# A two-layer decoder trunk on one core: where the softmax probabilities are transposed

## The chip, the cores and the metric

One core of one Trainium2 chip. The metric is device microseconds of one execution; the kernel before takes 770.55 us (median of 3 runs, 770.55 to 770.92).

## The reference

Two decoder layers over 528 tokens (16 meta tokens ahead of 512) of width 1024. Each layer normalises, makes one wide projection, and runs two token mixers side by side: a causal pooling and a latent attention with 8 heads. What this case turns on is the attention:

```
s = einsum('bqhd,bkhd->bhqk', q, k) * scale          # head width 96
s = where(causal, s, -1e30)
p = softmax(s, axis=-1)
o = einsum('bhqk,bkhd->bqhd', p, v)                  # value width 64
y_mla = (o * silu(z_mla)) @ w_mla_up
x = x + (sigmoid(g_pool) * y_pool + sigmoid(g_mla) * y_mla) @ w_out
```

Everything is float32.

## The kernel before, in words

**Products in three passes.** A float32 operand is split into a high part that TensorE takes in one pass (`fp32r`) and a low part, the rest. `split` (L274) does it: ScalarE copies the high part (L275), VectorE subtracts (L276). `mm3` (L180) then multiplies high by high, high by low and low by high (L181 to L183). Weights come in chunks of 128x512: `wload` (L170) fetches a chunk by SyncE's DMA queue (SP, L114) into one of three `raw` tiles and splits it (L176 ScalarE, L177 VectorE) into one of three pairs `whi`, `wlo`.

**Two streams of work.** All projections of both layers are listed in `register`, in order, and `stream` (L190) is a generator that emits them piece by piece. Each piece reports planned nanoseconds. Activations lie with the feature on the partitions and the 528 tokens along a row, in two segments of 264 (layer 0) or one of 512 (layer 1, which drops the meta tokens). `go` (L1073) walks through a layer's special parts and between them draws from the stream: `gap` (L1070) draws `FILL` planned ns (2950 in layer 0, 2850 in layer 1), but stops at the projection `RESERVE` (`gm5`); `fill_now` draws a given amount. During the heads the stream holds the tiles of z_mla (4), g_pool (8) and g_mla (8), each of two chunks, each evacuated by VectorE and ScalarE (L549 to L552, L617 to L619, L971 and L972). The framework's scheduler then orders the instructions of each engine, so neighbours in the code may be shifted against each other; on each engine the order is fixed when the kernel is built.

**A head.** `prep` (L735) makes keys and queries of a head (VectorE L742 and L753, GpSimd L743, ScalarE L749, two DMAs L756, one broadcast load L733). `head` (L759) computes the scores of four blocks of 128 queries, with the queries on the partitions. `top` (L774) is a VectorE instruction that adds the mask, scales and finds each row's extreme; `expo` (L781) is ScalarE's exponential, which also sums the row. VectorE adds and inverts the sums (L826, L827). GpSimd multiplies the probabilities by the inverse: the 16 columns of the meta keys into `pm` (L832), the rest in place (L834).

The value product needs the keys on the partitions. `pv` (L837) has TensorE transpose ten 128x128 blocks a head against an identity (L859), three to seven into one PSUM tile; `split` takes them out of PSUM as `th` and `tl`. Four key blocks follow, each a product with both parts of the values (`both`, L872) and one with the low part of the probabilities (`low`, L876), 512, 384, 256 and 128 columns long. `hosts` slips the last scores of the next head between these products in layer 0. The meta columns of two heads are turned by four small VectorE transposes (L848) and split into the three 32-row bands of `racc` (L903 to L905). After an odd head, `part2` adds the product with the meta values (L922), multiplies by the gate `zms` (L926) and splits the result for the up projection.

`pv(prev)` of one head runs in three parts inside the next head's turn: the loop in `go` is `head(h)`, gap, `prep(h+1)`, rest of `pv(h-1)`, gap, with two more gaps inside `head`.

**Tiles.** Probabilities lie in `pa` (two buffers) and in `cq8` to `cq11` by odd and even head; squares for the norms in 16 tiles `sq`; PSUM has four `mm` tiles, three `S` tiles and one `o` tile.

Of the kernel before, what the change touches and what calls it, by code (L numbers as in the profile page):

```python
# [52 lines left out]
FILL = (2950.0, 2850.0)  # L53
RESERVE = ("gm5", "gm5")
# [3 lines left out]
WARM = 8  # L58

# [12 lines left out]
def trunk(ctx, tc, xT, xrow, mrow, pos, win, wkr, wqb, wkb, wvb, wgr, wpu, wmu, wout, gains, const, yT):  # L72
# [23 lines left out]
    def sqt():  # L96
        return tp.tile([P, HALF], F32, tag="sq", name=nm("sq"), bufs=16)
# [72 lines left out]
    def wload(src, n, spare):  # L170
        raw = early.pop(0) if early else fetch(src, n, rawt(), sp)
        loads[0] += 1
        pool, th, tl, nb = (tp, "th", "tl", 2) if loads[0] <= 2 or spare else (wp, "whi", "wlo", 3)
        hi = pool.tile([P, W if pool is tp else 512], F32R, tag=th, name=nm("whi"), bufs=nb)
        lo = pool.tile([P, W if pool is tp else 512], F32R, tag=tl, name=nm("wlo"), bufs=nb)
        act.activation(hi[:, :n], raw[:, :n], AF.Copy)  # L176
        dve.tensor_sub(lo[:, :n], raw[:, :n], hi[:, :n].bitcast(F32))  # L177
        return hi, lo
# [134 lines left out]
    kdr = [dp.tile([H, T], F32, name=f"kdr{l}") for l in range(DEPTH)]  # L313

    hbuf = [(slot(f"hh{k}", F32R), slot(f"hl{k}", F32R)) for k in range(8)]

    class Layer:
        def __init__(self, l):
# [11 lines left out]
            self.sq = []  # L330
# [147 lines left out]
        def kr_rest(self, a, b):  # L478
# [5 lines left out]
            q = sqt()  # L484
# [82 lines left out]
        def mix(self, m, s):  # L567
# [7 lines left out]
            t = "tl" if m % 2 else "th"  # L575
            self.ys[m] = (slot(f"u{m}", F32R), tp.tile([P, W], F32R, tag=t, name=nm(t), bufs=2))
# [46 lines left out]
        def ev_k(self, p):  # L623
            def ev(ps, a, b):
# [6 lines left out]
                q = self.ksq[:, a:b] if p < 3 else sqt()[:, :b - a]  # L631
# [5 lines left out]
        def v_body(self, k, w):  # L637
# [17 lines left out]
            ps = mmt()  # L655
            for k in range(2):
                r = slot("pa", F32R, bufs=2, w=416)[:, 0:4 * NM].rearrange("p (a b) -> p a b", a=4)
# [18 lines left out]
        def q_stat(self, ps, a, b, c):  # L676
            for a0, b0 in FULL:
                a0, b0 = max(a, a0), min(b, b0)
                if a0 < b0:
                    q = sqt()  # L680
# [78 lines left out]
        def head(self, h, kq, prev):  # L759
# [7 lines left out]
            rs = sm.tile([P, 5], F32, tag="rs", name=nm("rs"), bufs=2)  # L767

# [17 lines left out]
            first = scores(1, s1, 0, 272)  # L786
            if self.hosted is not None:
                follow(first, self.hosted)
            scores(3, s3, 0, SPL)
            tops = [top(1, 1, s1, causal(272)), top(3, 4, s3, maskw[:, 0:SPL])]  # L790
# [3 lines left out]
            self.tops = tops + [top(2, 2, s2, causal(400))]  # L794
# [9 lines left out]
            scores(3, s4, SPL, T)  # L804
            def passes(out, q0, n):
# [3 lines left out]
            if self.last:  # L809
                scores(0, s0, 0, 144)  # L810
            else:
                sm_ = sc[0:NM, 432:432 + NM]
                todo = passes(s0, slice(NM, NM + P), 144) + passes(sm_, slice(0, NM), NM)
                if prev is None:
                    for fn in todo:
                        fn()
                else:
                    self.pv(prev, 1, todo)
# [6 lines left out]
            expo(0, 0, s0, pt[0])  # L825
            dve.tensor_add(rs[:, 3:4], rs[:, 3:4], rs[:, 4:5])  # L826
            dve.reciprocal(rs[:, 0:4], rs[:, 0:4])  # L827
            if odd == 0:
                self.pm = sm.tile([P, 4, 32], F32, tag="pm", name=nm("pm"), bufs=2)
# [7 lines left out]
        def pv(self, prev, part, hosts=()):  # L837
# [41 lines left out]
            def chain(*fns):  # L879
                last = None  # L880
                for fn in fns:
                    ins = fn()
                    if last is not None:
                        follow(ins, last)
# [332 lines left out]
```

## Time and profile before

| | |
|---|---|
| median of 3 runs | 770.55 us |
| span of the profiled execution | 768.5 us (its own time is not listed) |
| TensorE busy | 763.8 us |
| VectorE busy | 544.1 us |
| ScalarE busy | 408.9 us |
| GpSimd busy | 201.6 us |
| data moved by DMA | 84.05 MB, 109 GB/s |
| granted TensorE clock | 9 tenths or more of full speed in all 40 slices |

Times are microseconds of one profiled execution unless marked ns. PE is TensorE's matmuls, PEld its weight loads, DVE VectorE, ACT ScalarE, POOL GpSimd, SP or SPq SyncE with its DMA queue. L859 is line 859 of the kernel. A group is all instructions of one line, engine and shape: how many, their summed busy time, the mean of one in ns, then the idle time of the engine just before them and what ended it. A matmul's record runs from its start to its modelled end, and matmuls overlap: the price of one is the distance of starts. The chain that ended last is followed back from the last instruction, at each step to what released it.

### The profile page before, as it was taken

The numbers are of one execution on the slowest core, as the hardware profiler recorded it, in microseconds if no ns is written. First come the engines' busy times: TensorE is split into PE (matmuls) and PEld (weight loads), VectorE is DVE, ScalarE is ACT, GpSimd is POOL, SyncE is SP. The second block draws the span as 40 slices with busy tenths as digits, with TensorE's granted clock in tenths as the row PEclk, the third lists the DMA queues.
The fourth block names the chain that finished last, engine by engine and source line by source line (L and its number), as shares of the span: only waits on it lengthen the run. The fifth ranks groups of instructions, "written<-read, shape, count | busy, mean of one in ns | idle before, by whom it ended". The sixth has DMA issues, their size and how long they took to land.

```text
span 768.5 us, 14355 instructions
## 1 busy us (share of the span) xinstructions
PE 763.8 (99%) x5195; PEld 697.9 (91%) x5195; DVE 544.1 (71%) x1179; ACT 408.9 (53%) x892; POOL 201.6 (26%) x251
## 2 busy tenths in 40 slices
PE   9999999999999999999999999999999999999998
PEld 9999999999999999999997898887888888888887
DVE  5588687357899977785376486773677989775842
ACT  6755656545556665634264355454446666664320
POOL 2026204012242233052220262040132434420500
PEclk9999999999999999999999999999999999999999
DMA  8533233343223222325642333334433332222372
GB/s 293 160 113 98 75 97 98 104 141 105 89 79 91 84 71 70 107 71 169 178 133 97 110 86 89 96 87 127 125 119 90 94 93 77 82 69 70 119 222 98
DMA packets 54931, 84.05 MB, mean 109 GB/s; under 512 B 10006, under 2 KB 18582, under 8 KB 54860
## 3 DMA queue, kind: packets, MB, share of 16 engines
q1 hardware_dynamic: 54716, 82.87, 35.6%
q8 instruction: 41, 0.67, 0.4%
q14 instruction: 30, 0.25, 0.1%
q10 hardware_dynamic: 144, 0.26, 0.1%
HBM read 76.69 MB, written 4.29 MB: 105 GB/s over the span
## 4 chain that ended last, share of the span: by engine, by line
PE 99%; DMA 0%; ACT 0%; DVE 0%; SPq 0%; issue 0%; ACTq 0%
PE mm L181 29%; PE mm L183 29%; PE mm L182 29%; PE mm L859 2%; PE S L181 2%; PE S L182 2%; PE S L183 2%; PE o L876 1%; PE o L872 1%; PE S L503 1%; PE S L470 0%; DMA xb<-xT 0%; PE S L806 0%; PE mm L922 0%; PE mm L395 0%; PE S L872 0%
## 5 line engine op out<-in xcount | busy, mean ns | idle before, releaser
L181 PE MATMUL mm<-hh,whi 128*128 128x264 f32 (+2 forms) x1080 | 339.9, 317 | 0.0
L182 PE MATMUL mm<-hl,whi 128*128 128x264 f32 (+2 forms) x1080 | 338.2, 314 | 0.0
L183 PE MATMUL mm<-hh,wlo 128*128 128x264 f32 (+2 forms) x1080 | 337.1, 315 | 0.0
L177 DVE TENSOR_TENSOR wlo<-raw,whi 128x512 fp32r<-128x512 f32 (+2 forms) x251 | 186.7, 748 | 98.6 <-ACT whi L176 94.6
L176 ACT ACTIVATE whi<-raw 128x512 fp32r<-128x512 f32 (+2 forms) x251 | 150.2, 602 | 181.3 <-PE mm L182 135.3
L181 PEld LDWEIGHTS mm<-hh,whi 128*128 128x128 f32 x1080 | 202.5, 188 | 12.9 <-ACT kp L474 0.4
L182 PEld LDWEIGHTS mm<-hl,whi 128*128 128x128 f32 x1080 | 203.0, 188 | 12.2
L183 PEld LDWEIGHTS mm<-hh,wlo 128*128 128x128 f32 x1080 | 201.9, 188 | 12.2
L743 POOL TENSOR_TENSOR tmp<-kp,bc 64x528 f32<-64x528 f32 x16 | 25.6, 1600 | 123.9 <-PE mm L183 70.0
L604 POOL TENSOR_TENSOR racc<-racc,tmp 128x264 f32<-128x264 f32 (+1 forms) x15 | 14.3, 956 | 133.1 <-ACT tmp L603 133.1
L832 POOL TENSOR_TENSOR pm<-pa,rs 128x16 f32<-128x16 f32 x32 | 9.1, 285 | 126.1 <-DVE rs L827 126.1
L982 POOL TENSOR_TENSOR tmp<-tmp,xb 128x264 f32<-128x264 f32 (+1 forms) x24 | 26.9, 1138 | 56.0 <-DVE tmp L980 55.9
L774 DVE CUSTOM_DVE_ANT_0 S<-S,maskw,nqs 128x400 f32<-128x400 f32 (+4 forms) x80 | 38.4, 499 | 4.4 <-PE S L183 4.0
L781 ACT ACTIVATE cq<-S,bia 128x400 f32<-128x400 f32 (+2 forms) x48 | 24.6, 516 | 27.1 <-DVE bia L774 18.1
L181 PE MATMUL mm<-u,whi 128*128 128x264 f32 (+1 forms) x108 | 34.7, 322 | 0.0
L181 PE MATMUL mm<-cq,whi 128*128 128x264 f32 (+1 forms) x108 | 34.7, 321 | 0.0
L183 PE MATMUL mm<-u,wlo 128*128 128x264 f32 (+1 forms) x108 | 34.7, 321 | 0.0
L183 PE MATMUL mm<-cq,wlo 128*128 128x264 f32 (+1 forms) x108 | 34.5, 321 | 0.0
L182 PE MATMUL mm<-cq,whi 128*128 128x264 f32 (+1 forms) x108 | 34.5, 321 | 0.0
L834 POOL TENSOR_TENSOR cq<-cq,rs 128x384 f32<-128x384 f32 (+1 forms) x32 | 32.8, 1024 | 0.0
L276 DVE TENSOR_TENSOR tl<-mm,th 128x384 fp32r<-128x384 f32 (+1 forms) x48 | 27.9, 596 | 5.0 <-ACT th L275 4.8
L275 ACT ACTIVATE th<-mm 128x384 fp32r<-128x384 f32 (+1 forms) x48 | 24.1, 523 | 10.2 <-PE mm L859 9.2
(270 smaller groups left out, 1378.6 us busy)
## 6 DMA issues: line engine op xcount, KB each, us to landing
raw<-win SPq DMA_DIRECT2D x143, 256.0 KB, 2.6
raw<-wout SPq DMA_DIRECT2D x32, 256.0 KB, 3.0
bc<-kdr SPq DMA_DIRECT2D x16, 264.0 KB, 3.6
raw<-wpu SPq DMA_DIRECT2D x16, 256.0 KB, 2.7
raw<-wmu SPq DMA_DIRECT2D x16, 256.0 KB, 2.7
raw<-wqb SPq DMA_DIRECT2D x12, 256.0 KB, 2.6
xb<-xT SPq DMA_DIRECT2D x8, 264.0 KB, 5.7
tmp<-xT SPq DMA_DIRECT2D x16, 132.0 KB, 3.4
```

What stands on the lines that cost most here:

```text
L176: act.activation(hi[:, :n], raw[:, :n], AF.Copy)
L177: dve.tensor_sub(lo[:, :n], raw[:, :n], hi[:, :n].bitcast(F32))
L181: first = pe.matmul(out, wh, xh, start=start, stop=False)
L182: pe.matmul(out, wh, xl, start=False, stop=False)
L183: newest[0] = pe.matmul(out, wl, xh, start=False, stop=stop)
L275: act.activation(hi[:, a:b], src, AF.Copy)
L276: return dve.tensor_sub(lo[:, a:b], src, hi[:, a:b].bitcast(F32))
L743: gp.tensor_mul(kf[r0:r0 + 64, :], self.kp[r0:r0 + 64, :], bc[r0:r0 + 64, :])]
L774: return dve.tensor_tensor_reduce(out=sv, in0=sv, in1=mask, scale=nqs[:, i, h:h + 1], scalar=3e38, op0=ALU.add, op1=ALU.min, accum_out=bia ...
L781: act.activation(pv, sv, AF.Exp, scale=-1.0, bias=bia[:, i:i + 1], accum_out=rs[:, c:c + 1])
L834: gp.tensor_mul(pt[i][:, NM:], pt[i][:, NM:], rs[:, i:i + 1].to_broadcast([P, n - NM]))
L982: gp.tensor_add(t[:, :b - a], t[:, :b - a], self.am[m][:, a:b])
```

## The change

TensorE's transposes go. When a block row of probabilities is ready, `turn` lets VectorE transpose it in 32x32 blocks into the tile `attD`. Four DMAs store that tile to DRAM so that the blocks come to lie as rows of keys, and one DMA loads the 128x1280 result as `attE`. `parts` splits it from SBUF, in two halves, into `hi` (a wide `th` tile) and in place. `pv` reads its operands from these two with a stride: runs of 32 columns.

The probabilities are no longer divided by their row sums. The inverse sums go to DRAM (`rdr`) and come back as a broadcast over 64 partitions (`rb`); after an odd head GpSimd multiplies the gate `zms` by them. The meta columns are copied unscaled by GpSimd, turned by one VectorE transpose a pair of heads, split, and laid out by four DMAs through `mdr`.

`FILL` falls to 2620 and 2530, `RESERVE` becomes `gm3`, and `hosts` is no longer used. `attD` has one buffer, `attE` two. To make room, `pa` has one buffer, `cq8` and `cq10` serve all heads, the squares use `xb`, `attD` and `attE` (`halves`), and pairs of `th`, `tl` tiles become one wide tile. In the last part of a layer, `parts` and `pv` of head 7 have a `fill_now(2600)` ahead of each.

```diff
-FILL = (2950.0, 2850.0)
-RESERVE = ("gm5", "gm5")
+FILL = (2620.0, 2530.0)
+RESERVE = ("gm3", "gm3")
+NB = 10
+def block(i, j):
+    return 2 * i + j if j < 2 else 1 if i == 2 else 6 + j
...
+    def att(tag):
+        return sl.tile([P, NB * P], F32 if tag == "D" else F32R, tag=f"att{tag}", name=nm(f"att{tag}"), bufs=1 if tag == "D" else 2)
+
+    def wide():
+        return tp.tile([P, NB * P], F32R, tag="th", name=nm("th"), bufs=2)
...
+    pdr = [dp.tile([P, NB * P], F32, name=f"pdr{i}") for i in range(2)]
+    mdr = [dp.tile([P, 2 * P], F32, name="mdr")]
+    rdr = [[dp.tile([1, SEQ], F32, name=f"rdr{l}{h}") for h in range(H)] for l in range(DEPTH)]
...
-            pa = slot("pa", bufs=2, w=416)
-            pb = slot(f"cq{8 + odd}")
-            pc = slot(f"cq{10 + odd}")
+            pa, pb, pc = slot("pa", w=416), slot("cq8"), slot("cq10")
+            blocks = att("D")
+            grid = blocks.rearrange("p (b s r) -> p b s r", b=4, s=NB)
+            def turn(i):
+                gp.tensor_copy(pm[:, i, 16 * odd:16 * odd + 16], pt[i][:, 0:NM])
+                for j, n in ((0, i + 1),) if i in (0, 1, 3) else ((0, 2), (2, 1)):
+                    k = block(i, j)
+                    dve.transpose(grid[:, :, k:k + n, :].rearrange("p b s r -> p s b r"), pt[i][:, NM + P * j:NM + P * (j + n)])
...
             expo(1, 1, s1, pt[1])
             expo(2, 2, s2, pt[2])
+            turn(1)
+            turn(2)
             self.gap()
-            self.pv(prev, 0)
-            if self.last:
-                self.pv(prev, 1)
+            self.parts(prev)
             self.gap()
...
             expo(0, 0, s0, pt[0])
+            turn(3)
+            turn(0)
             dve.tensor_add(rs[:, 3:4], rs[:, 3:4], rs[:, 4:5])
             dve.reciprocal(rs[:, 0:4], rs[:, 0:4])
-            for i in range(4):
-                n = pt[i].shape[1]
-                gp.tensor_mul(self.pm[:, i, 16 * odd:16 * odd + 16], pt[i][:, 0:NM],
-                              rs[:, i:i + 1].to_broadcast([P, NM]))
-                gp.tensor_mul(pt[i][:, NM:], pt[i][:, NM:], rs[:, i:i + 1].to_broadcast([P, n - NM]))
+            row = rdr[self.l][h]
+            sp.dma_start(row.rearrange("a (p i) -> p (a i)", i=4), rs[:, 0:4])
+            got = att("E")
+            n = NB * 32
+            via = pdr[h % 2]
+            for a in range(4):
+                sp.dma_start(via[:, n * a:n * a + n].rearrange("(b k) x -> k b x", k=32),
+                             blocks[32 * a:32 * a + 32, :].rearrange("p (b x) -> p b x", x=n))
+            sp.dma_start(got.bitcast(F32), via)
+            sp.dma_start(rb[64 * odd:64 * odd + 64, 0:512], row.partition_broadcast(64))
+            if odd == 1:
+                self.meta_turn(pm)
+                z = self.zms[h // 2][:, NM:T].rearrange("p (i q) -> p i q", i=4)
+                gp.tensor_mul(z, z, rb[:, 0:512].rearrange("p (q i) -> p i q", i=4))
...
+        def parts(self, prev):
+            h, got = prev
+            hi = wide()
+            f = got.bitcast(F32)
+            for a in (0, NB * 64):
+                split(hi, got, f[:, a:a + NB * 64], a, a + NB * 64)
+            self.pt = hi, got
...
-                        pe.transpose(tr[:, c:c + P], pt[i][:, NM + P * j:NM + P * (j + 1)], ident)
...
+            for j in range(4):
+                k0, n = block(j, j), 4 - j
+                st = block(j + 1, j) - k0 if n > 1 else 1
+                hi, lo = (t.rearrange("p (a s r) -> p s a r", a=4, s=NB)[:, k0:k0 + st * (n - 1) + 1:st] for t in self.pt)
+                chain(pe.matmul(o[:, P * j:512], vt[:, j, h, :], hi, start=j == 0, stop=j == 3))
+                chain(pe.matmul(o[0:64, P * j:512], vt[:, j, h, 0:64], lo, start=False, stop=j == 3, skip_group_check=True))
...
-            fill_now(1300)
-            self.pv(prev, 0)
             if not self.last:
                 self.meta_queries()
             fill_now(2600)
-            self.pv(prev, 2)
+            self.parts(prev)
+            fill_now(2600)
+            self.pv(prev)
             up("gm7")
```

More of the change, by code (lines that the diff above doesn't have):

```diff
@@ L172, in wload @@
         loads[0] += 1
-        pool, th, tl, nb = (tp, "th", "tl", 2) if loads[0] <= 2 or spare else (wp, "whi", "wlo", 3)
-        hi = pool.tile([P, W if pool is tp else 512], F32R, tag=th, name=nm("whi"), bufs=nb)
-        lo = pool.tile([P, W if pool is tp else 512], F32R, tag=tl, name=nm("wlo"), bufs=nb)
+        if loads[0] <= 2 or spare:
+            t = wide()
+            hi, lo = t[:, 0:512], t[:, 512:1024]
+        else:
+            hi, lo = (wp.tile([P, 512], F32R, tag=t, name=nm(t), bufs=3) for t in ("whi", "wlo"))
         act.activation(hi[:, :n], raw[:, :n], AF.Copy)
@@ L900, in pv @@
-            if odd == 1 and part == (0 if final else 2):
-                self.mt = slot("racc", F32R)
-                v = lambda g: self.mt[g:g + 32, 0:512].rearrange("p (i c r) -> p c i r", i=4, c=4)
-                act.activation(v(0), self.turn, AF.Copy)
-                dve.tensor_sub(v(32), self.turn, v(0).bitcast(F32))
-                act.activation(v(64), self.turn, AF.Copy)
-            if part < 2:
-                return
-            t = turned((2, 3))
-            chain(lambda: both(2, t, 0), lambda: ready(t, lambda: both(3, t, 256)), lambda: low(3, t, 256), lambda: low(2, t, 0))
+            h, got = prev
@@ L1116, in go @@
             for h in range(H):
[L1117 removed]
+                now = self.head(h, kq, prev)
                 self.gap()
```

157 lines of the change are left out of this document (66 added, 91 removed).

## Prediction

> **What bounds the kernel now.** I read the page first: the shares of busy time, then the chain that ended last.
>
> ```profile
> span 768.5 us, 14355 instructions
> ...
> PE 763.8 (99%) x5195; PEld 697.9 (91%) x5195; DVE 544.1 (71%) x1179; ACT 408.9 (53%) x892; POOL 201.6 (26%) x251
> ...
> PE 99%; DMA 0%; ACT 0%; DVE 0%; SPq 0%; issue 0%; ACTq 0%
> ```
>
> TensorE idles for 4.7 us of 768.5, and the chain lies on it from end to end. Any work that leaves TensorE shortens the run, as long as nothing else makes TensorE wait. So the first question is what leaves. The chain in order of time tells it (start, length, what), and the groups of instructions give the count:
>
> ```profile
> by line: PE mm L181 28.7%; PE mm L183 28.6%; PE mm L182 28.5%; PE mm L859 2.3%; PE S L181 2.1%; PE S L182 2.0%; PE S L183 2.0%; PE o L876 1.1%; PE o L872 1.1%; PE S L503 0.7%; PE S L470 0.5%; DMA xb<-xT 0.4%; PE S L806 0.3%; PE mm L922 0.2%
> ...
> 198.57 0.33 PE mm L859 x3
> 207.11 0.77 PE mm L859 x7
> ...
> 224.75 0.44 PE mm L859 x4
> ```
> ```profile
> L859 PE MATMUL mm<-cst,cq 128*128 128x128 f32 x112 | 20.4, 272 | 0.0
> ...
> L859 PE MATMUL mm<-cst,pa 128*128 128x128 f32 x48 | 10.3, 272 | 0.0
> ```
>
> L859 is the transpose. Three take 0.33 us of the chain, four 0.44, seven 0.77: **0.11 us each**. The group's mean of 272 ns is one instruction from start to end; they overlap, so it is not the price.
>
> The second question is which engine comes next. Windows over the middle of the two head loops (columns: length, then busy time of PE, PEld, DVE, ACT, POOL, clock, DMA):
>
> ```profile
> 200.00:280.00 80.00, 80.00 (x664) 79.71 (x664) 73.24 (x175) 49.88 (x120) 28.41 (x43) 1.00 0.28 84
> 580.00:660.00 80.00, 80.00 (x420) 67.37 (x419) 71.64 (x161) 50.56 (x118) 31.84 (x45) 1.00 0.30 88
> ```
>
> There VectorE is busy 92% and 90%, against 71% over the span. The change puts its new work just there. ScalarE has 37% to spare.
>
> **The change part by part.** *Transposes leave TensorE.* 112 + 48 = 160 of them at 0.11 us: **-17.6 us**, the chain's 2.3% of 768.5. The seven `low` products that layer 0 split into two halves become one each again, with the same columns: nothing. Value products keep their columns (2 x 1280 a head); their moving operand now comes in runs of 32 columns. No row has such an operand. Bounds: nothing, or twice the price. I take nothing, since the runs are in the same memory and the array still takes one column after another; the other end is a rival.
>
> *Planned work moves.* The loop's four gaps a head shrink by 330 (layer 0) and 320 planner-ns (layer 1). Six matmuls that the planner books at 660 ns take 0.74 us:
>
> ```profile
> 379.73 0.29 PE L181 MATMUL mm<-hh,whi 128*128 128x264 f32 x1
> ...
> 380.47 0.28 PE L181 MATMUL mm<-hh,whi 128*128 128x264 f32 x1
> ```
>
> So a head loses 4 x 0.33 x 1.12 = 1.48 us of projections (1.43 in layer 1). They run behind the loop instead, where they cover the last head. For TensorE that is nothing; for VectorE it makes the loop denser. The reciprocal of each head marks the period, seven heads lying between the first and the last of a layer:
>
> ```profile
> 183.23 0.18 DVE L827 RECIPROCAL rs<-rs 128x4 f32<-128x4 f32 x1
> ...
> 304.13 0.18 DVE L827 RECIPROCAL rs<-rs 128x4 f32<-128x4 f32 x1 [0.20 <-ACT pa L781]
> ...
> 570.20 0.18 DVE L827 RECIPROCAL rs<-rs 128x4 f32<-128x4 f32 x1 [0.17 <-ACT pa L781]
> ...
> 682.10 0.18 DVE L827 RECIPROCAL rs<-rs 128x4 f32<-128x4 f32 x1 [0.20 <-ACT pa L781]
> ```
>
> Period 17.27 us in layer 0 and 15.99 in layer 1. TensorE's part after the change: 17.27 - 1.10 - 1.48 = 14.7, and 15.99 - 1.10 - 1.43 = 13.5 us.
>
> *VectorE's side*, from groups of the loop of layer 0 (181 to 320 us) and two of the whole span (L712 and the second L276 group):
>
> ```profile
> L177 DVE TENSOR_TENSOR wlo<-raw,whi 128x512 fp32r<-128x512 f32 x37 | 28.6, 773 | 8.1 <-ACT whi L176 7.9
> L619 DVE SCALAR_TENSOR_TENSOR xb<-tmp,xb 128x264 f32<-128x264 f32 x16 | 9.2, 573 | 0.8 <-ACT tmp L618 0.8
> ...
> L617 DVE TENSOR_TENSOR tmp<-mm,rinv 128x264 f32<-128x264 f32 x16 | 6.7, 425 | 0.2
> ...
> L848 DVE STREAM_TRANSPOSE srows<-pm 32x128 f32<-32x128 f32 x16 | 4.8, 299 | 0.3
> ...
> L904 DVE TENSOR_TENSOR racc<-srows,racc 32x512 fp32r<-32x512 f32 x4 | 2.7, 682 | 0.5 <-ACT racc L903 0.4
> ```
> ```profile
> L276 DVE TENSOR_TENSOR tl<-mm,th 128x384 fp32r<-128x384 f32 (+1 forms) x48 | 27.9, 596 | 5.0 <-ACT th L275 4.8
> ...
> L712 DVE STREAM_TRANSPOSE tmp<-srows 32x512 f32<-32x512 f32 x2 | 1.4, 680 | 0.0
> ```
>
> - Added a head: five block transposes, 1280 columns together. The two transpose rows give (680 - 299)/384 = 0.99 ns a column and 0.17 us fixed: 5 x 0.17 + 1.27 = 2.1 us. They have 32 partitions, the new ones 128; bounds are this and four times it, and I take the row, since other instructions here cost by columns alone.
> - The three low parts (27.9/16 = 1.74 us a head) become two of 640 columns, 2 x 0.83 = 1.66.
> - A pair of heads loses four small transposes (1.20) and L904 (0.68), and gains one of 128 columns (0.30) and a split (about 0.25): -0.66 a head.
> - Sum: **+1.4 us a head**.
> - The filler that leaves takes its VectorE work along: a weight chunk is 24 matmuls, 2.96 us, and with it L177 and, for z_mla and g_pool, one m-tile's worth of L617 and L619 halved, 0.77 + 1.00. That is 0.6 of its length: -0.9 us a head.
> - GpSimd's scaling of the probabilities goes as well, and it slows VectorE:
>
> ```profile
> 241.74 0.41 DVE L619 SCALAR_TENSOR_TENSOR xb<-tmp,xb 128x264 f32<-128x264 f32 x1
> ...
> 243.70 0.68 DVE L177 TENSOR_TENSOR wlo<-raw,whi 128x512 fp32r<-128x512 f32 x1
> ```
> ```profile
> 247.22 1.71 DVE L177 TENSOR_TENSOR wlo<-raw,whi 128x512 fp32r<-128x512 f32 x1
> ```
> ```profile
> 247.04 1.34 POOL L743 TENSOR_TENSOR tmp<-kp,bc 64x528 f32<-64x528 f32 x1 [5.31 <-DVE xb L619]
> ```
>
> The same subtraction takes 0.68 us alone and 1.71 beside a GpSimd product. Mean less undisturbed, over L177 (773 to 680, 4.6 a head) and L619 (573 to 410, two a head), is some 0.8 us a head; about half of GpSimd's work in the loop goes: -0.4. The Trainium skill (GPSIMD Engine Reference, section 8, Key points) says that GpSimd shares its SBUF interfaces with VectorE and gets in the way of instructions with two SBUF inputs; by that rule all of L834's share would come back, and the sum would be 0.4 us a head better.
>
> Layer 0: 0.916 x 17.27 = 15.8, + 1.4 - 0.9 - 0.4 = 15.9 us of VectorE against 14.7 of TensorE. Layer 1: 0.896 x 15.99 = 14.3, + 0.1 = 14.4 against 13.5. **VectorE becomes the longer one, by 1.2 and 0.9 us a head**, as long as the filler is z_mla and g_pool: 12 tiles of two chunks, 71 us, some five full heads. That is 6.0 + 4.5 = 10.5 us. Not all of it is waited for: three split weight tiles and four PSUM tiles hold about two chunks, 5.9 us, and the backlog drains in g_mla, which has one VectorE pass less. I let half of the hold count, 3 us a layer: **+4.5 us**. Bounds: 0 (a window at 95% lost nothing) and 10.5.
>
> *The way through DRAM.* A head's probabilities reach the value product after four stores, a load of 640 KB and a split. In the built kernel's order of instructions, 35,808 to 52,944 columns of matmuls lie between a head's last score and its first value product; by the matmul rows above (0.37 us for 3 x 264) that is 16.7 to 24.7 us. What the chain needs:
>
> ```profile
> 251.07 0.52 DVE L774 CUSTOM_DVE_ANT_0 S<-S,maskw,nqs 128x288 f32<-128x288 f32 x1
> ...
> 254.14 0.18 DVE L827 RECIPROCAL rs<-rs 128x4 f32<-128x4 f32 x1
> ```
> ```profile
> raw<-win SPq DMA_DIRECT2D x143, 256.0 KB, 2.6
> ...
> scr<-xb SPq DMA_DIRECT2D x8, 132.0 KB, 3.2
> ...
> qhl<-q SPq DMA_DIRECT2D x16, 64.0 KB, 2.1
> ...
> raw<-wkb SPq DMA_DIRECT2D x8, 128.0 KB, 2.1
> ```
> ```profile
> L733 SPq DMA_DIRECT2D bc<-kdr x16: 326/332/532, 160.1 to 618.2; - x16
> ```
> ```profile
> L176 ACT ACTIVATE whi<-raw 128x512 fp32r<-128x512 f32 (+2 forms) x251 | 150.2, 602 | 181.3 <-PE mm L182 135.3
> ```
>
> Masks and exponentials 3.1; two transposes 1.0; four stores issued and landed 3.4 (4 x 0.33 + 2.1) to 5.4; the load 4.1 (128 KB more costs 0.5) to 7.8 (three of 2.6); ScalarE's copies, 2 x 640 columns, 1.5: 13.1 to 18.8 us. I take 15, nearer the single transfers: under 16.7, so nothing. Weight loads queue behind these DMAs on SP for some 5 us a head; ScalarE waits 135 us for TensorE to free split weights, so they are ahead by more than that: nothing, or up to 2.6 us for a chunk without that cover.
>
> *The rest.* Row sums now go by DRAM to z_mla, needed only behind the value product, over 16 us later; two landings (5.3 to 6 us) are hidden. Single buffers for the probabilities wait for transposes that are done two gaps (5.8 us) earlier; shared scratch for the squares and the wide tiles add no instructions: nothing.
>
> **Sum.** 768.5 - 17.6 + 4.5 = 755.4 in the profile; 2.05 lie around it (770.55 median less the span; the profiled execution's own time is not listed): 757.5. I say **758**.
>
> **Rivals.**
> 1. *All hidden.* VectorE's 95% windows without a wait speak for it, the 15.9 against 14.7 against it. 770.55 - 17.6 = 753.
> 2. *The round trip comes late; slower.* The first value product waits in TensorE's queue and holds all projections behind it. VectorE with a backlog delays masks, transposes and splits in turn, and seven hops of 1 us would make 13.1 into 20. From the built order, a chain of 20.2 us costs as much as the transposes saved, 21 us costs 26: 779. Against it: the bound from rows ends at 18.8. The Trainium skill (VectorE: DVE Perf Modes, Rules for kernel authors) speaks for this side: for 128x128 it sends one to TensorE where PSUM will do, as VectorE turns 32x32 blocks only. By that rule the change loses, and the time would be this rival's; no run here shows it yet.
> 3. *The strided operand.* Twice the price for 2560 columns a head is 1.2 us, 19 us in all: 772, and the change does not relieve TensorE. Against it: nothing in the trace slows by operand.
>
> **How the numbers follow.** Forecast (VectorE sets the pace for part of the loop, 754.5 to 766) 0.45; hidden 0.23; round trip late 0.24, of which 0.2 ends slower; strided 0.08, most of it within 0.2%, which is 1.5 us and about what a measurement can tell from no change. Faster 0.71, same 0.07, slower 0.22. The range 752.5 to 775 takes in both bounds of VectorE's cost, the strided case and the mild end of the late one.
>
> **What would show it.** L859 gone and TensorE's busy time near 746 us: step one. VectorE over 95% busy in the loops, TensorE idle 3 to 10 us with VectorE named as the releaser: the forecast. Idle before the value products, released by the load or its split: rival 2. Value products longer than 0.4 us at 512 columns: rival 3. Transposes of 512 columns far from 0.68 us would break VectorE's sum, and the load landing after 8 us the chain's.

## The result and the profile after

The changed kernel takes **800.48 us** (median of 4, 799.54 to 802.79) against 770.73 us for the kernel before in the same session: a ratio of 1.0384, 95% interval 1.0364 to 1.0405. Forecast were 758 us and a range up to 775. The profiled execution took 800.05 us, of which 798.3 are its span; the mean granted clock of TensorE is 0.987 in it. One execution of a later version, 1042.77 us at a granted clock of 0.655, is left out of that version's median (760.73). The page after, with the shares of busy time and of the chain that ended last, and four rows of that chain (start, length, what):

```profile
span 798.3 us, 14211 instructions
...
PE 766.5 (96%) x5028; PEld 692.4 (87%) x5028; DVE 553.7 (69%) x1219; ACT 397.1 (50%) x868; POOL 166.4 (21%) x195
...
PE 10%; DMA 1%; DVE 1%; SPq 0%; issue 0%; ACT 0%; DVEq 0%
```
```profile
707.39 3.56 DMA pdr<-attD
...
711.14 4.42 DMA attE<-pdr
...
716.23 0.73 ACT th L295
...
717.00 0.60 PE S L918
```

TensorE has 167 instructions less (5195 to 5028), as meant, and yet is busy for 2.7 us more than before. It idles for 31.8 us (798.3 - 766.5) where it idled for 4.7. The chain can be followed back only to 694.80 us, over the last 13% of the span (the shares above add up to that), and there it no longer lies on TensorE alone: for the last head it runs from the stores (`pdr<-attD`) over the load (`attE<-pdr`) and ScalarE's copy to the value product. What happened before that is read from the waits. TensorE's waits (engine, instruction, what released it: total us, times, longest):

```profile
PE o L918 <- ACT th L295: 15.7, 11, 3.6
PE S L918 <- ACT th L295: 4.5, 2, 2.5
PE mm L203 <- DVE wlo L197: 3.5, 4, 1.3
PE mm L933 <- DMA racc<-mdr: 2.2, 2, 1.7
```

L918 is a head's first value product, L295 ScalarE's copy that makes the high part of the turned probabilities. So 20.2 us in 13 places are waits for the turned probabilities. What holds that copy, and VectorE's subtraction behind it, stands in the waits of those two engines:

```profile
ACT th L295 <- DMA attE<-pdr: 60.3, 16, 7.1
DVE attE L296 <- ACT th L295: 39.8, 14, 5.0
```

All 16 heads wait for the load from DRAM. ScalarE and VectorE work in a fixed order, so while they wait they do nothing else: 60 and 40 us.

One head shows the whole way. These are rows of the timeline of all engines (start, length, engine, what, idle time before it and its releaser), from the end of a head's scores at 193.4 to its first value product at 216.4:

```profile
193.16 0.28 PE L841 MATMUL S<-kh,qhl 128*128 128x144 f32 x2
...
195.37 1.37 ACT L295 ACTIVATE th<-attE 128x640 fp32r<-128x640 f32 x2 [3.23 <-DMA attE<-pdr]
...
196.15 0.82 DVE L296 TENSOR_TENSOR attE<-attE,th 128x640 fp32r<-128x640 f32 x1 [3.05 <-ACT th L295]
...
200.28 0.37 DVE L803 CUSTOM_DVE_ANT_0 S<-S,maskw,nqs 128x144 f32<-128x144 f32 x1
...
202.87 0.29 DVE L816 STREAM_TRANSPOSE attD<-pa 128x128 f32<-128x128 f32 x1
...
205.28 0.70 SPq L868 DMA_DIRECT2D pdr<-attD  x1
...
210.12 0.45 SPq L870 DMA_DIRECT2D attE<-pdr  x1
...
215.03 0.74 ACT L295 ACTIVATE th<-attE 128x640 fp32r<-128x640 f32 x1 [5.42 <-DMA attE<-pdr]
...
216.44 0.80 PE L918 MATMUL o<-th,vt 128*128 128x512 f32 x1 [3.62 <-ACT th L295]
```

The head's scores are done at 193.4, but VectorE masks their last row only at 200.28, 6.8 us later: until 196.15 it stood before the subtraction of the head *before*, whose load was late, and then it had a backlog. The turn ends at 203.2, the last store is issued at 205.28 to 206.0, the load leaves at 210.12 and releases the copy at 215.03. The value product follows at 216.44, 23.0 us behind the scores, and TensorE had nothing to do for 3.62 us. The mean over the 16 heads, from the same rows of each, is 24.1 us: scores to last mask 6.9, to the end of the last turn 4.9, to the load's issue 5.9, to the copy 4.9, to the product 1.5 (rounded).

The wait has a second price. Windows of TensorE around it (stretch, length, busy time and matmuls, granted clock, DMA share, GB/s):

```profile
212.00:213.00 1.00, 0.82 (x7) 1.00 0.81 323
213.00:216.40 3.40, 0.00 (x0) 0.87 1.08 292
216.40:218.00 1.60, 1.56 (x6) 0.50 0.22 55
218.00:220.00 2.00, 2.00 (x11) 0.50 0.00 0
220.00:222.00 2.00, 2.00 (x9) 0.50 0.39 139
222.00:224.00 2.00, 2.00 (x18) 0.92 0.39 112
...
321.28:324.28 3.00, 3.00 (x12) 0.50 0.15 57
```

After the wait the granted clock is 0.50 for almost 6 us, and in two stretches of 2 us only 11 and 9 matmuls start where 18 do at 0.92. The Trainium skill (TensorE: Matmul & The Clock Gate, "Why this matters for your kernels") says that a gap of more than about 3 us between matmuls brings the clock back to half; this row agrees. Other waits here do not keep to 3 us: behind one of 2.48 us the clock was 0.50 as well (the last row, which starts where that wait ends), and behind one of 2.78 us in a run below (the control, up to 257.35 us) it stayed at 1.00.

### The profile page after: what moved, and what is told of

It reads as the page before. It is cut to its first block, busy times and chain, and to the rows that moved or that the text cites. A ratio compares the mean times of both kernels' runs of the same rounds, so it can differ in the third digit from the quotient of the medians.

```text
span 798.3 us, 14211 instructions
## 1 busy us (share of the span) xinstructions
PE 766.5 (96%) x5028; PEld 692.4 (87%) x5028; DVE 553.7 (69%) x1219; ACT 397.1 (50%) x868; POOL 166.4 (21%) x195
## 2 busy tenths in 40 slices
DMA packets 74642, 109.76 MB, mean 138 GB/s; under 512 B 14358, under 2 KB 35222, under 8 KB 74572
## 5 line engine op out<-in xcount | busy, mean ns | idle before, releaser
L197 DVE TENSOR_TENSOR wlo<-raw,whi 128x512 fp32r<-128x512 f32 (+2 forms) x242 | 175.0, 727 | 89.2 <-ACT whi L196 85.6
L196 ACT ACTIVATE whi<-raw 128x512 fp32r<-128x512 f32 (+2 forms) x242 | 144.1, 599 | 152.3 <-PE mm L202 124.3
L202 PEld LDWEIGHTS mm<-hl,whi 128*128 128x128 f32 x1072 | 203.6, 190 | 13.1
L296 DVE TENSOR_TENSOR attE<-attE,th 128x640 fp32r<-128x640 f32 x32 | 30.5, 972 | 39.8 <-ACT th L295 39.8
L295 ACT ACTIVATE th<-attE 128x640 fp32r<-128x640 f32 x32 | 21.9, 729 | 60.3 <-DMA attE<-pdr 60.3
L813 POOL COPY pm<-cq 128x16 f32<-128x16 f32 x32 | 13.5, 423 | 141.4 <-ACT cq L810 140.6
L803 DVE CUSTOM_DVE_ANT_0 S<-S,maskw,nqs 128x240 f32<-128x240 f32 (+4 forms) x80 | 37.6, 492 | 5.2 <-PE S L203 4.6
L202 PE MATMUL mm<-th,whi 128*128 128x264 f32 (+1 forms) x108 | 34.6, 321 | 0.0
```

The costliest lines, as they stand in the source:

```text
L202: pe.matmul(out, wh, xl, start=False, stop=False)
L295: act.activation(hi[:, a:b], src, AF.Copy)
L296: return dve.tensor_sub(lo[:, a:b], src, hi[:, a:b].bitcast(F32))
L803: return dve.tensor_tensor_reduce(out=sv, in0=sv, in1=mask, scale=nqs[:, i, h:h + 1], scalar=3e38, op0=ALU.add, op1=ALU.min, accum_out=bia ...
```

## The experiments

Theory 1: the way through DRAM takes longer than the columns that TensorE has in front of the value product, and as the split sits in the fixed order of ScalarE and VectorE, a late load delays the next head's masks, too. ("Columns" are the matmuls between a head's last scores and its value product in TensorE's order, counted at 0.462 ns a column; the prediction's six matmuls of 264 columns in 0.74 us give nearly the same.) Theory 2: VectorE is the bound, by its transposes. Theory 3: the order in SyncE's queue delays the load. Lines of the experiments' kernels are a few off from those above.

**No way through DRAM.** The turned tile also gets two buffers, and the split's low part one.

```diff
-            got = att("E")
...
-            sp.dma_start(got.bitcast(F32), via)
+            got = blocks
```

> The changed kernel without the five transfers a head that carry the turned blocks through DRAM: VectorE turns the blocks into a tile from which the split reads at once, so the exchange of 32-row groups between partitions is left out (the values are not the reference's). VectorE's transposes, the split, the two value products and the row sums behind the product all stay. Theory 1 (the way through DRAM, some 11 us from the last turn to the split's start, held by engines that work in a fixed order, makes the period of a head longer than TensorE's work): TensorE's idle time falls from 31.8 us to under 10, the half-clock stretches go, and the time is 753 to 760 us. Theory 2 (VectorE, with 2.05 us of transposes more a head, is the bound): it stays at 785 us or more. Theory 3 (the broadcast of the row sums holds up SyncE's queue ahead of the load): as theory 1, since the load that it delays is gone.

Measured: 759.87 us (one execution). Its page, and windows over the two head loops (length, then busy time of PE, PEld, DVE, ACT, POOL, clock):

```profile
span 757.9 us, 14074 instructions
...
PE 750.1 (99%) x5028; PEld 682.7 (90%) x5028; DVE 552.8 (73%) x1219; ACT 399.4 (53%) x868; POOL 163.5 (22%) x195
```
```profile
200.00:280.00 80.00, 79.39 (x636) 77.72 (x635) 78.29 (x194) 48.30 (x119) 19.13 (x28) 1.00 0.36 101
580.00:660.00 80.00, 78.01 (x385) 65.16 (x385) 79.11 (x181) 49.32 (x115) 19.31 (x29) 1.00 0.39 107
```

With all transposes still on VectorE the span is 40.4 us shorter than that of the changed kernel, TensorE idles for 7.8 us, and its clock is 1.00 in both loops. VectorE is busy for 98 and 99% of the loops and hardly makes TensorE wait. The value product does not even have more columns in front of it: they are 16.7 us in the mean, counted from the matmul rows, against 20.2 in the changed kernel, and still none of the 16 waits for the split. The way through DRAM is the cause; theory 2 falls as the main one.

**No turns, the way stays.** Two kernels; the second has two buffers for the stored tile and one for the loaded one.

```diff
...
-                    dve.transpose(grid[:, :, k:k + n, :].rearrange("p b s r -> p s b r"), pt[i][:, NM + P * j:NM + P * (j + n)])
-            pt = [pa[:, 0:144], pa[:, 144:416], pb[:, 0:400], pc[:, 0:T]]
+            pt = [blocks[:, 0:144], blocks[:, 144:416], blocks[:, 416:816], blocks[:, 816:1344]]
```

> The changed kernel without VectorE's transposes: the exponentials are written into the tile that the stores read, and all five transfers a head stay with the same sizes (the transposing is left out, the values are not the reference's). VectorE has 2.05 us a head less, 33 us in all. Theory 1: the way through DRAM still sets the period and is shortened only by the last block row's two turns, about 0.3 to 0.7 us a head, 5 to 11 us in all: 785 to 797 us. Theory 2: most of the loss comes back, under 770 us. Theory 3: as theory 1.

> As the run without VectorE's transposes, but with two buffers for the tile that the exponentials write and one for the load's, since in that run the exponentials waited 24.8 us for the stores of the head before. The transposing is left out again, the values are not the reference's. Theory 1: the way through DRAM still sets the period, 785 to 797 us. Theory 2: under 770 us.

Measured: 805.86 and 812.80 us (one execution each). Neither theory had them slower than the changed kernel. They turned out inconclusive: with the transposes gone, the scheduler also placed the value product 2.7 us of columns earlier in TensorE's order (17.6 us behind the last scores instead of 20.3, counted in the built order at 0.462 ns a column). So the order was held in a later pair, a control with the turns and a kernel without: the value product stands behind the gap, its first matmul behind the last 40 weight groups issued ahead of it.

```diff
+                self.gap()
                 self.pv(prev)
                 prev = now
-                self.gap()
```

> The control for the run beside it: the changed kernel with each value product held behind the projections issued ahead of it, so that TensorE has 20.9 us of columns (at 0.462 ns a column) between a head's last scores and its value product, against 20.3 us in the changed kernel; the split stays where it was. Theory 1: the way takes some 24 us and the columns grew by 0.6 us only, so nearly all of the loss stays: 788 to 800 us. Theory 2: no change, 797 to 802 us.

> The control without VectorE's transposes (left out: the transposing; the values are not the reference's), with two buffers for the tile that the exponentials write. In the two runs without transposes so far the first value product also moved ahead in TensorE's order, to 17.6 us of columns behind the last scores; here it is held where the control has it, at 19.8 us. Theory 1: the way through DRAM still ends last, and is shorter by the last two turns only, less the 1.1 us of columns that are missing: within 10 us of the control. Theory 2 (VectorE's 33 us of transposes make the loss): 20 us or more under the control.

Measured: 802.15 us for the control (ratio 1.0412, 1.0376 to 1.0448), 816.13 without turns (1.0593, 1.0572 to 1.0615). The waits of ScalarE and VectorE before the split, of the control and then of the kernel without turns, beside VectorE's busy time in the page:

```profile
ACT th L297 <- DMA attE<-pdr: 57.8, 16, 6.8
...
DVE attE L298 <- ACT th L297: 39.0, 14, 5.1
```
```profile
ACT th L297 <- DMA attE<-pdr: 81.8, 16, 7.2
DVE attE L298 <- ACT th L297: 73.0, 16, 8.3
```
```profile
PE 766.5 (96%) x5028; PEld 691.2 (87%) x5028; DVE 554.3 (69%) x1219; ACT 397.0 (50%) x868; POOL 165.7 (21%) x195
```
```profile
PE 771.4 (95%) x5028; PEld 695.2 (85%) x5028; DVE 526.7 (65%) x1139; ACT 398.7 (49%) x868; POOL 166.1 (20%) x195
```

VectorE has 27.6 us less to do, and waits for the split 34.0 us longer. What was taken from it came back as waiting, and the masks came no earlier. Theory 2 is refuted in the presence of the way through DRAM. Why the kernel without turns is slower than its control is not settled; it has 1.1 us of columns a head less, but the two runs before it do not line up by columns.

**VectorE's work alone, on the kernel before.**

```diff
+            for i, a, b in ((1, 0, 256), (2, 0, 256), (2, 256, 384), (3, 0, 256), (3, 256, 512), (0, 0, 128)):
+                dve.transpose(bin_[:, 0:b - a], pt[i][:, NM + a:NM + b])
```

> The kernel before with six transposes a head on VectorE besides (the same blocks, turned into a scratch tile that nothing reads); TensorE's transposes and everything else stay. VectorE has some 2 us a head more, 33 us in all. Theory 1: the kernel before has no way through DRAM, and its engines have slack to take up VectorE's work: 770 to 775 us. Theory 2: if VectorE's work alone made the loss, it shows here too: 785 us or more.

Measured: 778.65 us (one execution) beside 771.29: 7.4 us, between the two forecasts. TensorE's largest new wait there:

```profile
PE mm L862 <- POOL pa L837: 3.4, 3, 2.7
```

It stands before TensorE's transposes, which wait for GpSimd's scaling, which waits for VectorE's row sums: a path that the changed kernel no longer has. VectorE's work is not free: on this kernel it costs a quarter of the loss, part of it by that path. What it would cost by itself in the changed kernel is not shown by this run.

**The row sums alone, on the kernel before.**

```diff
-                gp.tensor_mul(pt[i][:, NM:], pt[i][:, NM:], rs[:, i:i + 1].to_broadcast([P, n - NM]))
...
+            sp.dma_start(row.rearrange("a (p i) -> p (a i)", i=4), rs[:, 0:4])
...
+                sp.dma_start(rb[64 * odd:64 * odd + 64, 0:256], row[:, 256 * k:256 * k + 256].partition_broadcast(64))
```

> The kernel before with the second half of the change alone: TensorE goes on turning the probabilities, unscaled, and the row sums go through DRAM to the gate as in the changed kernel, in two tiles. GpSimd loses five multiplications a head (201.6 us busy goes to about 165), TensorE's work stays. Every theory puts the loss into the turning of the probabilities and not here: 766 to 773 us. If the row sums' own way through DRAM cost the time, it would be 780 us or more here too.

Measured: 772.21 us (one execution); the kernel before ran from 770.18 to 772.80 beside it. No loss can be told.

**The load ahead of the row sums in SyncE's queue.**

```diff
-            sp.dma_start(row.rearrange("a (p i) -> p (a i)", i=4), rs[:, 0:4])
...
             sp.dma_start(got.bitcast(F32), via)
+            sp.dma_start(row.rearrange("a (p i) -> p (a i)", i=4), rs[:, 0:4])
```

> The changed kernel with SyncE's order of issue turned round: the store of the row sums and their broadcast behind the four stores and the load of the blocks, so that the load waits for nothing but the stores. The whole computation stays. Theory 3 (the waits in SyncE's queue, 21.1 us for the row sums' store in 14 places and 10.2 us for the blocks' stores in 11, delay the load): the period shortens by 1 to 1.5 us a head, and the time falls to 775 to 785 us. Theory 1: the load leaves at most 0.3 us sooner, because the stores of the blocks wait for the last turn anyway: 793 to 800 us. Theory 2: no change.

Measured: 802.44 us (one execution). That lies within the changed kernel's own runs (799.54 to 802.79): theory 3 falls. The load leaves 5.4 us behind the last turn in the mean instead of 5.9, and the way from scores to product is 24.1 us as before.

**One hop.**

```diff
-                sp.dma_start(via[:, n * a:n * a + n].rearrange("(b k) x -> k b x", k=32),
-                             blocks[32 * a:32 * a + 32, :].rearrange("p (b x) -> p b x", x=n))
-            sp.dma_start(got.bitcast(F32), via)
+                for b in range(4):
+                    sp.dma_start(got[32 * b:32 * b + 32, n * a:n * a + n].bitcast(F32), blocks[32 * a:32 * a + 32, n * b:n * b + n])
```

> The changed kernel in its own order of work, with one hop in place of two: 16 transfers a head (32 partitions x 320 values each) go from the turned blocks straight into the partitions of the split's source, with nothing written to DRAM between. The whole computation stays. Theory 1: the way from the last turn to the split becomes shorter by a landing and the wait between (2.1 to 3 us, and 12 more issues cost some of it), and since that way sets the period, 1.5 to 3 us a head come back: 760 to 780 us. Theory 2 (VectorE's own work is the bound): no change, 795 to 802 us. Theory 3 (the order in SyncE's queue): no change or worse, since the queue has 11 more issues a head.

Measured: 841.05 us, ratio 1.0887 (1.0852 to 1.0921). Theories 1 and 2 missed it; theory 3 had a loss by more issues, though none so large. A row of SyncE's timeline, and a wait of ScalarE:

```profile
200.85 9.18 SPq L868 DMA_DIRECT2D attE<-attD  x14
```
```profile
ACT whi L196 <- DMA raw<-win: 46.0, 30, 5.0
```

Fourteen issues take 9.18 us of SyncE's queue, 0.66 us each. What the hop saved is lost to issuing, and the queue carries the weights too: ScalarE waits 46.0 us for these raw weights (`raw<-win`) where it waited 3.8 in the changed kernel. The way is counted in issues as well as in hops. This run says little on theory 1.

**The split later.** It leaves the middle of a head for the place behind the next head's preparation, its copies behind the head's last exponential and its subtractions behind the last turn.

```diff
-            self.parts(prev)
...
-                split(hi, got, f[:, a:a + NB * 64], a, a + NB * 64)
+                b = a + NB * 64
+                follow(act.activation(hi[:, a:b], f[:, a:b], AF.Copy), self.last_exp)
+                follow(dve.tensor_sub(got[:, a:b], f[:, a:b], hi[:, a:b].bitcast(F32)), self.last_turn)
...
+                self.parts(prev)
+                self.gap()
                 self.pv(prev)
                 prev = now
-                self.gap()
```

> The whole computation of the changed kernel, with one thing moved: the split of head h-1 on ScalarE and VectorE, and its value product on TensorE, are put one half step later, the split behind the last exponential and the last turn of head h, the value product behind the first two score rows of head h+1. A late load then blocks no mask and no exponential, and TensorE has some 22 to 33 us of columns between the last scores and the value product rather than 17 to 25. Theory 1: the loop is broken, TensorE's idle time falls under 12 us, 753 to 765 us. Theory 2 (VectorE is the bound): its work is the same, so little changes, 790 us or more. Theory 3: the load is as late as before, but there is more time for it: between 765 and 790 us.

Measured: 782.09 us, ratio 1.0129 (1.0083 to 1.0176). Some 60% of the loss is gone (11.6 of 29.8 us are left) with the same work on every engine; theory 2 is out by this run as well, and theory 1 had expected more. The waits of TensorE and the two engines:

```profile
PE S L919 <- ACT th L897: 11.6, 2, 7.3
```
```profile
ACT th L897 <- DMA attE<-pdr: 18.9, 4, 6.5
...
DVE attE L898 <- ACT th L897: 15.6, 3, 6.6
```

Of TensorE's 21.0 us of idle time 11.6 now lie at two places, the last head of each layer, where no further head covers the way. ScalarE and VectorE wait in 4 and 3 places instead of 16 and 14, and over the heads the last scores are masked 4.1 us after they are done, not 6.9: 4.1 is also the mean without the way through DRAM. The 2.8 us more are what these two runs lack and the changed kernel has: engines that stand before a late load with the next masks behind them. But the run moves the value product as well: TensorE has 24.6 us of columns in front of it in the mean, not 20.2, and the way is no shorter (some 26 us). How much of the 18 us regained is due to the loop and how much to the longer cover, this run does not tell.

**The layers' ends.** Fillers cut a little between heads, and more columns ahead of what still waits: first 12,500 units of projections before the last head's product, then 8000 (two kernels), then 9500 and 10,000. From the two kernels on the meta tokens' products and each pair's second product are held back as well. In all of them the last head's value product stands behind the last 40 weight groups issued ahead of it. The diff is that of the last step, against the changed kernel and without the later split.

```diff
-FILL = (2620.0, 2530.0)
+FILL = (2570.0, 2400.0)
...
-                after((3 if p == 3 else 2) * LAG, part2)
+                after((5.5 if p == 3 else 4.5) * LAG, part2)
...
-            after(2 * LAG, rest)
+            after(6 * LAG, rest)
...
-            fill_now(2600)
+            fill_now((9500, 10000)[self.l])
```

> The kernel with the later split, and beside it the end of each layer's head loop filled: the fillers between heads are cut from 2620 and 2530 to 2470 and 2380 units, and 12,500 units of projections rather than 2600 stand ahead of the last head's value product. With the later split 11.6 of TensorE's 21.0 us of idle time lie in two waits, at the last value product of each layer, and its matmuls took some 13 us longer than the products at full clock. Theory 1 (a latency that TensorE must have columns to cover, with the half clock behind each long wait): both waits go, and the time is 753 to 760 us, under the kernel before. Theory 2 (VectorE is the bound): the waits move to other heads, and it stays near 780 us.

Measured: 787.38 us (1.0189 to 1.0235): worse than the split later alone. The waits at the last product went, but a longer one came behind it:

```profile
306.86 0.99 PE L969 MATMUL mm<-mh,vb 96*128 96x16 f32 x4 [9.34 <-DVE mh L963]
```

The meta tokens' product had lost the columns that were moved ahead. Theory 1's number failed; its rule fits, if each waiting product needs columns of its own.

> The later split with a milder filling of each layer's end than the run before: fillers of 2550 and 2440 units between heads, 8000 rather than 12,500 units ahead of the last head's value product, and more distance for what follows it (the meta tokens' products 10,000 rather than 4000 units behind, each pair's second product 6000 and the last 8000 rather than 4000 and 6000). In the run with 12,500 units the two waits at the last value products were gone, but 9.3 us of waiting stood ahead of the meta tokens' product (for VectorE) and 6.3 us ahead of the pairs' second products (for the meta weights' load). Theory 1 (a latency that needs columns of TensorE's work in front of each waiting product, wherever it stands): idle under 12 us and 758 to 768 us. Theory 2 (VectorE is the bound, and the waits only move): 780 us or more.

> As the run beside it, with the first layer's filler at 2620 units, the meta tokens' product 12,000 units behind, and each head's value product (not the last's alone) held behind the 40 weight groups issued ahead of it. Theory 1: 758 to 768 us as well, the two within 4 us of each other. Theory 2: 780 us or more.

Measured: 772.03 us (ratio 0.9991 to 1.0031) and 772.16 (1.0006 to 1.0048), the two alike, each some 4 us over what theory 1 expected, and level with the kernel before.

> The later split with the milder filling, and more columns at the places where the best run so far still waited (3.9 us of TensorE's idle time before the meta tokens' products, 2.1 us at the last value products): fillers of 2570 and 2400 units, 9500 and 10,000 units ahead of the last value product, second products 9000 and 11,000 units behind, the meta tokens' product 12,000. Theory 1: what is left of the waits goes, 760 to 768 us, under the kernel before. Theory 2: 770 us or more.

> As the run beside it, and in SyncE's queue the store and loads of the meta tokens' weights stand ahead of the second head's broadcast of the row sums, which waits for the row sums' store to land. Theory 3 (waits in SyncE's queue matter where a product waits for what is queued behind them): 1 to 3 us less than the run beside it. Theory 1: the same within 2 us, if the columns already cover the meta tokens' way; both 758 to 768 us.

> The kernel of the run before it once more, in more rounds, since its profiled execution there was a disturbed one: 759 to 764 us, 0.98 to 0.99 of the kernel before, TensorE's idle time under 8 us (theory 1). Theory 2 has no such time: 770 us or more.

Measured: 763.29 us (0.9872 to 0.9925) and 760.73 (0.9857 to 0.9890), and the second once more 762.57 (0.989, 0.9869 to 0.9910). **This version computes everything the changed kernel does and beats both**, the kernel before by 1.1% and the changed one (800.48) by 4.7%. It also moves as much by DMA as the changed kernel (109.77 and 109.76 MB, 84.05 in the kernel before), so it was not the bytes that cost the time. Whether the queue's order is worth anything in it stays unclear: the intervals of the first two overlap. Its page and TensorE's first wait, from the last run:

```profile
span 761.1 us, 14227 instructions
...
PE 752.2 (99%) x5028; PEld 683.8 (90%) x5028; DVE 553.4 (73%) x1219; ACT 396.8 (52%) x868; POOL 171.5 (23%) x195
```
```profile
PE o L922 <- ACT th L900: 2.8, 2, 2.2
```

The way itself is no shorter, 24.8 us from scores to value product by the same rows as above; but TensorE has 24.2 us of columns in front of it in the mean, not 20.2, and of the 20.2 us of waiting for the high part 2.8 are left.

## Why the prediction was wrong, by its own steps

1. *Transposes leave TensorE, -17.6 us.* Right in kind, too large: in the run without the way through DRAM TensorE is busy for 750.1 us, not 763.8, so -13.7, or 0.086 us a transpose and not 0.11. The chain's rows gave too high a price; the distance of starts in the kernel before gives the right one:

```profile
198.41 0.49 PE L859 MATMUL mm<-cst,cq 128*128 128x128 f32 x3
198.66 0.37 PE L181 MATMUL mm<-hh,whi 128*128 128x264 f32 x1
```

   Three transposes start within 0.25 us, 0.083 us each, and over all 160 the distances from a transpose to the next matmul add up to 13.2 us.
2. *Value products at no extra cost.* Right; the rival of the strided operand is out. The same product before, and then in the run without the way, both read in groups by shape (busy, mean ns):

```profile
L872 PE MATMUL o<-th,vt 128*128 128x512 f32 x14 | 5.6, 399 | 0.0
```
```profile
L912 PE MATMUL o<-th,vt 128*128 128x512 f32 x14 | 5.6, 397 | 0.0
```

   By the distance of starts it is 0.23 us in both, too (a chain row at 228.85 us in the kernel before, the starts at 210.12 and 210.35 us in the run without the way).

3. *VectorE, +1.4 us a head and +4.5 us in all.* The durations held: the transposes of the changed kernel, by shape,

```profile
L816 DVE STREAM_TRANSPOSE attD<-cq 128x512 f32<-128x512 f32 x16 | 11.2, 702 | 0.1
L816 DVE STREAM_TRANSPOSE attD<-cq 128x256 f32<-128x256 f32 x16 | 6.9, 430 | 1.3 <-ACT cq L810 0.7 <-ACT pa L810 0.6
L816 DVE STREAM_TRANSPOSE attD<-pa 128x256 f32<-128x256 f32 x16 | 6.8, 428 | 5.2 <-DMA pdr<-attD 5.1
L816 DVE STREAM_TRANSPOSE attD<-pa 128x128 f32<-128x128 f32 x16 | 4.8, 297 | 0.0
L816 DVE STREAM_TRANSPOSE attD<-cq 128x128 f32<-128x128 f32 x16 | 4.3, 268 | 0.0
```

   are 34.0 us together, 2.1 a head, as worked out from rows of 32 partitions. VectorE did come to its limit in the run without the way (99% of the loop of layer 1), and that run idles for 3.1 us more than the kernel before; so the term is 3.1 at most. In the changed kernel VectorE is not the pace: it waits 39.8 us.
4. *The way through DRAM: "I take 15, nearer the single transfers: under 16.7, so nothing."* **This is the step that failed.** It took 24.1 us in the mean, outside the bounds of 13.1 to 18.8. By its parts: load 4.9 (4.1 to 7.8 taken) and copies 1.5 (1.5) held. Masks, exponentials and turns took 4.9, not 4.1 (3.1 + 1.0); most of the difference is one head with 11.6, in which VectorE stood before a late split between its last mask and its last turn. The stores took 5.9 to the load's issue, not 3.4 to 5.4. And 6.9 us between the scores and their last mask were not in the sum at all: it starts at a mask and takes VectorE as free when the scores are done. The head whose masks it read shows otherwise in the kernel before:

```profile
248.73 0.24 PE L806 MATMUL S<-kh,qhl 128*128 128x144 f32 x2
...
252.13 0.36 DVE L774 CUSTOM_DVE_ANT_0 S<-S,maskw,nqs 128x144 f32<-128x144 f32 x1
```

   That stretch is 3.2 us here and 2.7 in the mean of the 16 heads, 4.1 in the run without the way, with the turns on VectorE, and 6.9 with both. The last 2.8 us are a loop: the split of the head before stands in VectorE's order ahead of these masks, so a late load makes the next load late. The step did not see the loop, but without it the way would by subtraction still be 21.3 us, beyond the bounds and beyond the 16.7 that it was compared with. The second rival named the loop's members ("delays masks, transposes and splits in turn"), and the prediction set the bound of 18.8 against it.
5. *The rest at nothing.* Right as far as one execution tells (772.21 for the row sums' way). What had no term is the single buffer of `attD`: VectorE waits 5.1 us for the stores that still read it (third row of the transposes).
6. *Not in the sum:* the clock. From the run without the way to the changed kernel, TensorE's busy time for the same matmuls grows from 750.1 to 766.5, 16.4 us. The mean granted clock of 0.987 accounts for some 10 of these at most (0.013 x 798.3); the other 6 are not assigned.

The account of the loss: -13.7 for the transposes, +27.1 for idle time (31.8 - 4.7), +16.4 for busy time at a lower clock and what else stretches it, together +29.8, which is 798.3 - 768.5. The second rival had the mechanism. Its 779 was too low: it reckoned with a way of 21 us where 24.1 were measured, and had no lower clock in it. The Trainium skill's rule for 128x128 transposes (VectorE: DVE Perf Modes, Rules for kernel authors) gave the right sign for the changed kernel (ratio 1.038), but the last version (0.989) shows that the order of work decided it and not the engine: with columns in front of the value product, turning outside TensorE is the faster way by 1.1%.

## What to carry to other kernels

When work leaves the bounding engine for a longer way round, count the way from the last producer (here the scores, not the first mask) to the first consumer with every engine's *queue* in it: in a fixed order an instruction that waits for this way holds up whatever the next turn of the same way needs. Compare it with the columns the bounding engine has in front of the consumer, at the last iteration as well, where nothing follows to cover it. A scheduler can undo the cover: in two runs here it put the value product 2.7 us of columns earlier. So hold the consumer's place, and look after each product that waits.

## What was not expected of the hardware

- A wait of 3.62 us left TensorE at a granted clock of 0.50 for some 6 us more, so that wait cost more than its length; one of 2.78 us did not.
- Sixteen transfers of 40 KB between partitions hold the issuing queue for 0.66 us each (14 in 9.18 us), where the load of 640 KB took 0.45 in the head above. Here one small transfer was dearer to issue than the large load; direction and shape differ too.
- VectorE ran at 98 and 99% of the two loops with TensorE at 99 and 98%: with two engines near their limits side by side, TensorE idled for 3.1 us more than in the kernel before, over the whole run.
